# A two-layer hybrid trunk on one core: closing norm with its offsets laid into the result first and rows added by their stores, two row blocks' statistics on ScalarE, the last gating ahead of the last weight splits

## The chip, the cores and the metric

The kernel runs on one core of one Trainium2 chip. The metric is the device time of one execution in microseconds (us); the median of three runs before the change is 1376.93 us (1375.47 to 1379.27). Engines are named as in the profile: PE is TensorE, DVE is VectorE, ACT is ScalarE, POOL is GpSimd, SP is the queue that issues the plain transfers.

## What is computed

512 tokens of width 1024 pass through two layers. Each layer is a mixer (sparse attention beside a short convolution) and a feed-forward part, each closed by a layer norm of ALPHA times its input plus its output. The first layer's feed-forward is dense; the second one's is a mixture of 8 experts of which each token takes the best two. The end of the second layer is what the change touches:

```python
def layer_norm(x, g, b):
    mu = jnp.mean(xf, -1, keepdims=True)
    var = jnp.mean(jnp.square(xf - mu), -1, keepdims=True)
    return ((xf - mu) * lax.rsqrt(var + LN_EPS) * g + b)
...
def moe_swiglu(h, w_router, wg, wu, wd):
    out = jnp.zeros_like(h)
    for e in range(N_EXPERTS):
        out = out + gate[..., e:e + 1] * swiglu(h, wg[e], wu[e], wd[e])
    return out
...
        f = moe_swiglu(h, ...)
        h = layer_norm(ALPHA * h + f, ln2_g[l], ln2_b[l])
    return h
```

## The kernel before

All matrix work is done in a split form: a weight block is copied to a short format (`whi`, on ACT) and what the copy loses is kept as a second block (`wlo`, on DVE, which needs `whi`); three products, high by high, high by low and low by high, then stand for one. `split16` does this for the experts' weights, with `split16_ops` issuing the two instructions.

In the second layer the tokens are routed, experts are sorted by how many tokens they have, and each expert gathers its tokens (`x` from `hbuf`), multiplies by `moe_wg` and `moe_wu` (`expert_up`, two column groups of 6 and 5 blocks of 128), gates (`expert_gate`, `expert_hidden`: `eg` is the gated product on DVE, `ehh` its short copy on ACT, `ehl` the remainder on DVE) and multiplies by `moe_wd` (`expert_down`, or `expert_down_rows` for experts of exactly 128 slots). An expert's rows are then added to `abuf`, a buffer in device memory that starts as the layer's input, by indirect transfers that add at their target (`add_rows`, issued by POOL). Each such transfer waits for the one before. `expert_out` prepares these rows for the experts with two chunks of slots: PE transposes four blocks into a bank, ACT scales the bank into `yr`, twice per chunk; both chunks use the banks named `mm` and `po`.

The last expert works differently. When its turn begins (`if last:` in `moe`), the other seven experts' sums are read back from `abuf`: four blocks of 128 rows into `h`, and the last expert's own rows by a gather into `xl`. While its final matrix work runs, DVE takes the statistics of the four blocks (`row_stats`, `bn_aggr`), one root on ACT serves all (`roots`), and `finish(0)` norms each block by two DVE instructions (`rows_scaled`: subtract the mean and multiply by the gain; multiply by the root and add the offset) and stores it plainly from SP. `last_rows` adds the last expert's product to `xl` and takes its statistics; these rows are normed after that and written over the stored ones by an indirect scatter (`out_dram<-xl,dst`), which waits for the four stores.

The order on each engine's queue is set by the recording layer: instructions stand in the order of their data and priorities, and `issue_after` holds one back until another has been placed.

Of the kernel before, what the change touches and what calls it, by code (L numbers as in the profile page):

```python
# [54 lines left out]
class Trunk:  # L55
# [562 lines left out]
    def route(self, l, mp):  # L618
# [9 lines left out]
        self.dst = mp.tile([128, NE, 2], I32, name="dst")  # L628
        self.sgate = mp.tile([128, NE, 2], F32, name="sgate")

    def route_tile(self, tt):
        nc = self.nc
        if tt == 0:
            self.xt = self.state.tile([128, KD, S], F32, name="xh")
            room = self.state.tile([128, KD * S], F32, name="xl")
            n16, n32 = NE * NT * CAP // 2, NT * CAPS[0]
            self.oh16 = room[:, 0:n16].bitcast(F16).rearrange("p (e t j) -> p e t j", e=NE, t=NT)
            self.oh32 = room[:, n16:n16 + n32].rearrange("p (t j) -> p t j", t=NT)
        xt = self.xt
        q = slice(tt * 128, tt * 128 + 128)  # L640
        if tt == NT - 1:
            self.first = [self.psum(tag) for tag in ("mm", "mm", "s")]
            for u in range(NT - 1):
                self.first_rows(u)
        for half in range(2):
            p = self.psum("tr")
            for k in range(4):
                kk = half * 4 + k
                nc.tensor.transpose(p[:, k * 128:(k + 1) * 128], self.h[:, tt, kk * 128:(kk + 1) * 128], self.ident)
            v = p.rearrange("p (k q) -> p k q", k=4)  # L650
            self.routed = [nc.scalar.activation(xt[:, half * 4:half * 4 + 4, q], v, AF.Copy)]
        p = self.psum("po")
        for k in range(KD):
            nc.tensor.matmul(p[:, 0:NE], xt[:, k, q], self.wr[:, k], start=k == 0, stop=k == KD - 1)
        lg, sel = self.lg[:, tt], self.selb[:, tt]
        nc.vector.tensor_copy(lg, p[:, 0:NE])
        other = lg[:, None, :].to_broadcast([128, NE, NE])
        own = lg[:, :, None].to_broadcast([128, NE, NE])
        a = self.small.tile([128, NE, NE], F32, name="ra", bufs=1)
        b = self.small.tile([128, NE, NE], F32, name="rb", bufs=1)  # L660
        nc.vector.tensor_tensor(a, other, own, op=OP.is_equal)
        nc.vector.tensor_tensor(a, a, self.nkeep8, op=OP.mult)
        nc.vector.tensor_tensor(b, other, own, op=OP.is_gt)
        nc.vector.tensor_tensor(a, a, b, op=OP.add)
        rank = self.small.tile([128, NE], F32, name="rank")
        nc.vector.tensor_reduce(rank, a, axis=AX.X, op=OP.add)
        nc.vector.tensor_scalar(sel, rank, 1.5, None, op0=OP.is_lt)

        p = self.psum("po")
        for u in range(tt + 1):  # L670
            nc.tensor.matmul(p[:, 0:NE], self.before if u == tt else self.ones, self.selb[:, u], start=u == 0, stop=u == tt)
        nc.vector.scalar_tensor_tensor(self.mark[:, tt], p[:, 0:NE], 1.0, sel, op0=OP.add, op1=OP.mult)
        self.routed.append(nc.vector.tensor_scalar(self.oh32[:, tt], self.slots[:, 0:CAPS[0]], self.mark[:, tt, 0:1], None,
                                                   op0=OP.is_equal))
        if tt == NT - 1:
            self.first_rows(tt)
# [151 lines left out]
    def split16_ops(self, st, hi, lo, n):  # L828
        nc = self.nc

        for c in (slice(0, n // 2), slice(n // 2, n)) if n > 1 and self.nblock < 3 else (slice(0, n),):
            nc.scalar.activation(hi[:, c], st[:, c], AF.Copy, scale=WS)  # L832
            self.low = nc.vector.scalar_tensor_tensor(lo[:, c], st[:, c], WS, hi[:, c], op0=OP.mult, op1=OP.subtract)  # L833

    def weights(self, name, i0, e, rows, cols):

# [31 lines left out]
    def expert_hidden(self, parts, g):  # L868
        nc = self.nc
        hh, hl = (self.mp.tile([128, 6 * CAP], F16, name=x, bufs=2) for x in ("ehh", "ehl"))  # L870
        for x, c in parts:
            nc.vector.scalar_tensor_tensor(g[:, c], x, HS / (XS * WS), g[:, c], op0=OP.mult, op1=OP.mult)
            nc.scalar.activation(hh[:, c], g[:, c], AF.Copy)
            nc.vector.tensor_tensor(hl[:, c], g[:, c], hh[:, c], op=OP.subtract)
        return hh, hl

    def expert_down(self, i0, e, f0, n, hh, hl, ys):
# [10 lines left out]
                             lambda k: (hi[:, k - k0, c], lo[:, k - k0, c], hh[:, r(k)], hl[:, r(k)]), k0, k1,  # L888
                             first=f0 + k0 == 0 and m == 0, last=f0 + k1 == NFE and m == nm - 1, shared=True)

    def expert_down_rows(self, i0, e, f0, n, hh, hl, ys, finish=None):

        held = []
        for k0 in range(0, n, 2):
            k1 = min(n, k0 + 2)
            src = self.weights("moe_wd", i0, e, slice((f0 + k0) * 128, (f0 + k1) * 128), slice(0, D))
            hi, lo = self.split16(self.eblock([128, k1 - k0, D], src))
            held += [(k0 + k, hi[:, k], lo[:, k]) for k in range(k1 - k0)]
            if finish is not None and 0 < k0 and k1 < n:
                continue  # L900
            for half, y in enumerate(ys):
                c = slice(half * 512, half * 512 + 512)
                for k, h, l in held:
                    r = slice(k * 128, k * 128 + 128)
                    for a, b in ((hh, h), (hl, h), (hh, l)):
                        self.nc.tensor.matmul(y, a[:, r], b[:, c], start=f0 + k == 0 and a is hh and b is h,  # L906
                                              stop=f0 + k == NFE - 1 and b is l)
                if finish is not None and k1 == n:
                    finish(half)
            held = []  # L910
# [27 lines left out]
    def expert_out(self, e, yt):  # L938
        nc = self.nc
        for r, (s, n) in enumerate(chunks(e)):  # L940
            yr = self.mp.tile([128, D], F32, name="yr", bufs=2)[0:n]
            for half in range(2):
                p = self.psum("po" if half else "mm")
                for k in range(4):
                    nc.tensor.transpose(p[0:n, k * 128:(k + 1) * 128], yt[:, half * 4 + k, s:s + n], self.ident)
                nc.scalar.activation(yr[:, half * 512:half * 512 + 512], p[0:n], AF.Copy, scale=self.sgate[0:n, e, r:r + 1])
# [17 lines left out]
    def moe(self, l):  # L964
        nc = self.nc
        mp = self.mp = self.pool("moe%d" % l)
        i0 = l // 2
        self.nblock = 0
        groups = [(0, 6), (6, 5)]
        xs = self.gather_t(0, None)  # L970
        self.aux = mp.tile([128, NT, NE, 5], F16, name="aux")
# [40 lines left out]
        for turn, e in enumerate(TURN):  # L1012
# [23 lines left out]
            mid = None if last else (lambda: nxt.extend(self.gather_t(after, xg)))  # L1036
            hid = self.expert_hidden(up("moe_wu", 1, mid=mid), gate)
            before, xs = (e, hid, ys), nxt

        with self.tc.issue_after(self.low.ins):  # L1040
            for tt in range(NT):
                nc.vector.bn_aggr(mv[:, tt], self.row_stats(self.h[:, tt]))
            rs = self.small.tile([128, NT, 1], F32, name="rs4")
            roots(rs, mv)
            nc.vector.tensor_tensor(self.bad[:, 0:NT], mv[:, :, 1], mv[:, :, 1], op=OP.not_equal)

        def finish(half):
            if half == 0:
                with self.tc.issue_after(self.low.ins):
                    for tt in range(NT):  # L1050
                        self.rows_scaled(self.h[:, tt], mv[:, tt, 0:1], rs[:, tt], gb)
                        self.store(tt)
            last_rows(half, ys[half])
        self.expert_down_rows(i0, final, *groups[1], *hid, ys, finish)

        nl, nh, xl = 128, 1, end[:, 2:3]
        mv2 = mp.tile([nl, nh, 2], F32, name="mv2")
# [135 lines left out]
```

## Time and profile before

| | |
|---|---|
| median of three runs | 1376.93 us |
| the profiled execution, its own time | 1376.29 us |
| its span, first to last instruction | 1374.5 us |
| PE busy | 1331.4 us (97%) |
| DVE busy | 865.7 us (63%) |
| ACT busy | 668.4 us (49%) |
| POOL busy | 76.5 us (6%) |
| share of PE in the chain that ended last | 90% |
| last product of the last `moe_wu` block ends | 1344.7 us |
| last expert's final scatter is issued | 1367.6 us |

The profiled execution took 1.8 us more than its span, and 0.6 us less than the median of the runs. Times on the trace are counted from the start of the span. The busy shares are means over the whole kernel; the last 30 us have other limits than the rest, and are read by themselves.

### The profile page before, as it was taken

To read this page: it belongs to the slowest core of one execution; us is meant where nothing else is said; L and a number is where in the kernel's file an instruction comes from. 1 tells how busy PE (TensorE), PEld (TensorE's weight loads), DVE (VectorE), ACT (ScalarE), POOL (GpSimd) and SP (SyncE) were. 2 spreads that over 40 slices of the span, in tenths; PEclk is the share of its full clock that TensorE was granted. 3 is DMA by queue.
4 is the path that set the end of the run, shared out by engine and by line. 5 is a ranking of instruction groups with operands and counts; after the bars stand their busy time and mean duration, and the time that the engine had idled before them with its cause. 6 is when DMAs were issued, how large, how long until landed. Compare 5 with 4: busy or idle time off the path is not lost.

```text
span 1374.5 us, 26819 instructions
## 1 busy us (share of the span) xinstructions
PE 1331.4 (97%) x11476; PEld 1156.4 (84%) x11476; DVE 865.7 (63%) x1250; ACT 668.4 (49%) x948; POOL 76.5 (6%) x85
## 2 busy tenths in 40 slices
PE   5999999999999999999999999999999999999994
PEld 5888788898888888888887888889999999999872
DVE  7567665743333332228566665759787787788897
ACT  3575543323223222113565444326677677687881
POOL 3000000000000000000000000101011011010130
PEclk9999999999999999999999999999999999999997
DMA  8442021332323223222552020758999899999992
GB/s 253 128 123 62 32 62 35 119 105 79 123 74 110 92 100 112 95 92 70 159 152 62 31 62 1 245 228 300 313 358 354 275 339 371 315 354 375 378 377 98
DMA packets 135806, 241.09 MB, mean 175 GB/s; under 512 B 10810, under 2 KB 80538, under 8 KB 135684
## 3 DMA queue, kind: packets, MB, share of 16 engines
q1 hardware_dynamic: 130868, 223.19, 47.7%
q0 software_dynamic: 4816, 16.17, 4.2%
q8 instruction: 90, 1.47, 0.4%
q14 instruction: 32, 0.26, 0.1%
HBM read 227.74 MB, written 11.68 MB: 174 GB/s over the span
## 4 chain that ended last, share of the span: by engine, by line
PE 90%; DVE 4%; DMA 2%; ACT 2%; issue 1%; SPq 0%; POOL 0%; POOLq 0%; ACTq 0%; DVEq 0%
PE mm L203 46%; PE s L203 16%; PE tr L203 10%; PE po L486 3%; PE s L504 2%; PE s L470 2%; PE s L378 1%; PE po L203 1%; PE tr L470 1%; PE tr L504 1%; PE s L906 1%; DVE h L961 1%; DMA abuf<-yr,dst 1%; DVE h L962 1%; DMA h<-abuf 1%
## 5 line engine op out<-in xcount | busy, mean ns | idle before, releaser
L203 PEld LDWEIGHTS <-whi 128*128 128x128 f16 x3872 | 311.5, 98 | 1.2
L147 ACT ACTIVATE whi<-stage 128x1024 fp32r<-128x1024 f32 x122 | 127.9, 1058 | 302.9 <-PE mm L203 187.4
L148 DVE TENSOR_TENSOR wlo<-stage,whi 128x1024 fp32r<-128x1024 f32 x118 | 143.6, 1223 | 195.2 <-ACT whi L147 192.8
L203 PE MATMUL mm<-xh,whi 128*128 128x512 f32 (+1 forms) x672 | 257.2, 383 | 0.3 <-DVE e L309 0.3
L203 PE MATMUL mm<-xh,wlo 128*128 128x512 f32 (+1 forms) x672 | 252.8, 376 | 0.4 <-DVE wlo L148 0.4
L203 PE MATMUL mm<-xl,whi 128*128 128x512 f32 (+1 forms) x672 | 252.0, 375 | 0.0
L833 DVE SCALAR_TENSOR_TENSOR wlo<-estage,whi 128x1536 f16<-128x1536 f32 (+4 forms) x106 | 201.7, 1918 | 37.4 <-ACT whi L832 37.3
L832 ACT ACTIVATE whi<-estage 128x1536 f16<-128x1536 f32 (+4 forms) x106 | 170.5, 1613 | 65.8 <-PE s L203 26.0
L203 PEld LDWEIGHTS <-wlo 128*128 128x128 f16 x1936 | 189.1, 98 | 0.0
L203 PEld LDWEIGHTS mm<-xh,wlo 128*128 128x128 f32 x672 | 126.8, 189 | 23.9 <-DVE wlo L148 0.6
L203 PEld LDWEIGHTS mm<-xh,whi 128*128 128x128 f32 x672 | 127.4, 190 | 21.7 <-issue 1.3
L203 PEld LDWEIGHTS mm<-xl,whi 128*128 128x128 f32 x672 | 127.1, 189 | 21.0
L203 PE MATMUL tr<-eh,whi 128*128 128x128 f16 (+6 forms) x704 | 133.0, 226 | 0.0
L203 PE MATMUL tr<-eh,wlo 128*128 128x128 f16 (+6 forms) x704 | 133.0, 226 | 0.0
L203 PE MATMUL tr<-el,whi 128*128 128x128 f16 (+6 forms) x704 | 133.0, 226 | 0.0
L203 PE MATMUL mm<-eh,whi 128*128 128x128 f16 (+6 forms) x704 | 132.3, 226 | 0.0
L203 PE MATMUL mm<-eh,wlo 128*128 128x128 f16 (+6 forms) x704 | 132.3, 226 | 0.0
L203 PE MATMUL mm<-el,whi 128*128 128x128 f16 (+6 forms) x704 | 132.3, 225 | 0.0
L833 DVE SCALAR_TENSOR_TENSOR wlo<-stage,whi 128x1536 f16<-128x1536 f32 (+5 forms) x56 | 102.5, 1840 | 22.3 <-ACT whi L832 22.2
L832 ACT ACTIVATE whi<-stage 128x1536 f16<-128x1536 f32 (+5 forms) x56 | 86.8, 1551 | 40.2 <-PE tr L203 15.6
L203 PE MATMUL s<-ehl,whi 128*128 128x160 f16 (+5 forms) x528 | 102.6, 228 | 0.0
L203 PE MATMUL s<-ehh,whi 128*128 128x160 f16 (+5 forms) x528 | 102.6, 228 | 0.0
(310 smaller groups left out, 2297.2 us busy)
## 6 DMA issues: line engine op xcount, KB each, us to landing
estage<-in_moe_wd_dram SPq DMA_DIRECT2D x29, 1024.0 KB, 7.6
stage<-in_w_in_dram SPq DMA_DIRECT2D x32, 512.0 KB, 5.2
estage<-in_moe_wu_dram SPq DMA_DIRECT2D x21, 768.0 KB, 8.5
estage<-in_moe_wg_dram SPq DMA_DIRECT2D x18, 768.0 KB, 7.0
stage<-in_ffn_wg_dram SPq DMA_DIRECT2D x11, 1024.0 KB, 5.4
stage<-in_ffn_wu_dram SPq DMA_DIRECT2D x11, 1024.0 KB, 5.1
stage<-in_ffn_wd_dram SPq DMA_DIRECT2D x11, 1024.0 KB, 4.9
stage<-in_moe_wd_dram SPq DMA_DIRECT2D x11, 1024.0 KB, 7.4
```

The source lines that it names most:

```text
L147: nc.scalar.activation(h, st, AF.Copy)
L148: (eng or nc.vector).tensor_tensor(o, st, h.bitcast(F32), op=OP.subtract)
L203: self.nc.tensor.matmul(p, a, b, start=first and n == 0, stop=last and n == total - 1, skip_group_check=shared)
L378: nc.tensor.matmul(ph[r:r + 64, 0:256], e2[kv][:, c].rearrange("p g n -> p (g n)"), w1s[c // 8][:, c % 8], start=c < 2, stop=c > 13, skip_ ...
L470: nc.tensor.transpose(q[:, k * 128:k * 128 + 128], flat[:, c:c + 128], self.ident)
L486: nc.tensor.matmul(po[g * 64:g * 64 + 64, i * 128:i * 128 + 128], v[:, j, c:c + 64], flat[:, k:k + 128], start=False, stop=lbr == 1 and j ...
L504: nc.tensor.matmul(sp[:, wide[i]], qs[:, a, g, qi[i]], keys[:, br, g, 0:wide[i].stop - wide[i].start], start=keys is ks and i == blocks[0] ...
L832: nc.scalar.activation(hi[:, c], st[:, c], AF.Copy, scale=WS)
L833: self.low = nc.vector.scalar_tensor_tensor(lo[:, c], st[:, c], WS, hi[:, c], op0=OP.mult, op1=OP.subtract)
L906: self.nc.tensor.matmul(y, a[:, r], b[:, c], start=f0 + k == 0 and a is hh and b is h, stop=f0 + k == NFE - 1 and b is l)
L961: self.nc.vector.scalar_tensor_tensor(x, x, mean, gb[0:m, 0], op0=OP.subtract, op1=OP.mult)
L962: self.nc.vector.scalar_tensor_tensor(x, x, rs, gb[0:m, 1], op0=OP.mult, op1=OP.add)
```

## The change

The closing norm of the four row blocks is done in another order. The offsets (`ln2_b`) are written into all 512 rows of the result by one plain transfer early in the program. Each block then gets (x - mean) * gain on DVE and a multiplication by its root on ACT, and is added to the result by an indirect transfer from POOL's queue that adds at its target (row numbers in the new tile `token`), where a plain store from SP stood. The statistics of blocks 2 and 3 move from DVE to ACT: a copy that also sums, a scaled negative of the sum, and a square that also sums. The roots are taken for two blocks at a time. The gating of the last expert's last column group is placed ahead of the second and third of its last weight splits. Apart from that, `expert_out` puts its second chunk into the `s` banks.

```diff
@@ route
+        self.token = mp.tile([128, NT], I32, name="token")
+        nc.gpsimd.iota(self.token, pattern=[[128, NT]], base=0, channel_multiplier=1)
+        b = t["ln2_b"][l]
+        nc.sync.dma_start(self.out[0], bass.AP(tensor=b.tensor, offset=b.offset, ap=[[0, S], [1, D]]))
@@ split16_ops
-            nc.scalar.activation(hi[:, c], st[:, c], AF.Copy, scale=WS)
-            self.low = nc.vector.scalar_tensor_tensor(lo[:, c], st[:, c], WS, hi[:, c], op0=OP.mult, op1=OP.subtract)
+            self.high = nc.scalar.activation(hi[:, c], st[:, c], AF.Copy, scale=WS)
+            with ExitStack() as ctx:
+                for ins in self.held:
+                    ctx.enter_context(self.tc.issue_after(ins.ins))
+                self.low = nc.vector.scalar_tensor_tensor(lo[:, c], st[:, c], WS, hi[:, c], op0=OP.mult, op1=OP.subtract)
@@ expert_down_rows
+            if first is not None and k0 == 0:
+                first()
@@ expert_out
-                p = self.psum("po" if half else "mm")
+                p = self.psum("s" if r else ("mm", "po")[half])
@@ moe
-        with self.tc.issue_after(self.low.ins):
-            for tt in range(NT):
-                nc.vector.bn_aggr(mv[:, tt], self.row_stats(self.h[:, tt]))
-            rs = self.small.tile([128, NT, 1], F32, name="rs4")
-            roots(rs, mv)
-            nc.vector.tensor_tensor(self.bad[:, 0:NT], mv[:, :, 1], mv[:, :, 1], op=OP.not_equal)
+        rs, nm = (self.small.tile([128, NT, 1], F32, name=x) for x in ("rs4", "nm4"))
+        up_done, hidden, main = self.low, self.rest, self.main
+
+        def row_sums():
+            with self.tc.issue_after(up_done.ins):
+                for tt in range(2):
+                    nc.vector.bn_aggr(mv[:, tt], self.row_stats(self.h[:, tt]))
+            self.held = (hidden,)
 
         def finish(half):
             if half == 0:
+
+                with self.tc.issue_after(self.high.ins), self.tc.issue_after(main.ins):
+                    for tt in (2, 3):
+                        junk = mp.tile([128, D], F32, name="yr", bufs=2)
+                        nc.scalar.activation(junk, self.h[:, tt], AF.Copy, accum_out=mv[:, tt, 0:1])
+                        nc.scalar.activation(nm[:, tt], mv[:, tt, 0:1], AF.Copy, scale=-1.0 / D)
+                        nc.scalar.activation(junk, self.h[:, tt], AF.Square, bias=nm[:, tt], accum_out=mv[:, tt, 1:2])
+                    nc.vector.tensor_scalar(mv[:, 2:4], mv[:, 2:4], 1.0 / D, None, op0=OP.mult)
+                    for tts in (slice(0, 2), slice(2, 4)):
+                        roots(rs[:, tts], mv[:, tts])
+                nc.vector.tensor_tensor(self.bad[:, 0:NT], mv[:, :, 1], mv[:, :, 1], op=OP.not_equal)
                 with self.tc.issue_after(self.low.ins):
                     for tt in range(NT):
-                        self.rows_scaled(self.h[:, tt], mv[:, tt, 0:1], rs[:, tt], gb)
-                        self.store(tt)
+                        x = self.h[:, tt]
+                        nc.vector.scalar_tensor_tensor(x, x, mv[:, tt, 0:1], gb[:, 0], op0=OP.subtract, op1=OP.mult)
+                        nc.scalar.activation(x, x, AF.Copy, scale=rs[:, tt])
+                        nc.gpsimd.indirect_dma_start(
+                            out=self.out[0], in_=x, in_offset=None, compute_op=OP.add,
+                            out_offset=bass.IndirectOffsetOnAxis(ap=self.token[:, tt:tt + 1], axis=0))
             last_rows(half, ys[half])
-        self.expert_down_rows(i0, final, *groups[1], *hid, ys, finish)
+        self.expert_down_rows(i0, final, *groups[1], *hid, ys, finish, row_sums)
+        self.held = ()
```

How the instructions stand now is shown at three places. A row is a source line, an operation, the written and read tiles and a size. First VectorE in the last expert's final stretch: `wlo` is a weight split, `eg` and `ehl` are the gating, `rs` the roots, `mv` the means, `h` the four blocks. Before:

```order
L955 BN_STATS st<-h 128x6
L833 SCALAR_TENSOR_TENSOR wlo<-estage,whi 128x2048
L1042 BN_AGGR mv_7452<-st 128x2
L833 SCALAR_TENSOR_TENSOR wlo<-estage,whi 128x2048
L872 SCALAR_TENSOR_TENSOR eg<-tr,eg 128x512
L872 SCALAR_TENSOR_TENSOR eg<-tr,eg 128x128
L982 RECIPROCAL rs_15109<-rs_15109 128x4
L1045 TENSOR_TENSOR bad<-mv_7452 128x4
L833 SCALAR_TENSOR_TENSOR wlo<-estage,whi 128x1024
L874 TENSOR_TENSOR ehl<-eg,ehh 128x512
```

and now:

```order
L841 SCALAR_TENSOR_TENSOR wlo<-estage,whi 128x2048
L1055 BN_AGGR mv_7455<-st 128x2
L880 SCALAR_TENSOR_TENSOR eg<-tr,eg 128x512
L880 SCALAR_TENSOR_TENSOR eg<-tr,eg 128x128
L882 TENSOR_TENSOR ehl<-eg,ehh 128x512
L882 TENSOR_TENSOR ehl<-eg,ehh 128x128
L841 SCALAR_TENSOR_TENSOR wlo<-estage,whi 128x2048
L841 SCALAR_TENSOR_TENSOR wlo<-estage,whi 128x1024
L992 RECIPROCAL rs_15096<-rs_15096 128x2
L1074 SCALAR_TENSOR_TENSOR h<-h,mv_7455,xl 128x1024
```

Both gating steps now stand ahead of the two last splits, and two blocks' statistics are gone from the rows ahead of them.

Next ScalarE in the same stretch, from the last weight split on. Before:

```order
L832 ACTIVATE whi<-estage 128x1024
L981 ACT_TABLE_LOAD
L981 ACTIVATE rs_15109<-mv_7452,eps 128x4
L873 ACTIVATE ehh<-eg 128x512
L873 ACTIVATE ehh<-eg 128x128
L981 ACTIVATE rs_15181<-mv_15178,eps 128x1
```

and now (`yr` takes a result that nobody reads, the sums go to `mv`; `nm` is the negative mean):

```order
L837 ACTIVATE whi<-estage 128x1024
L881 ACTIVATE ehh<-eg 128x512
L881 ACTIVATE ehh<-eg 128x128
L1064 ACTIVATE yr,mv_7455<-h 128x1024 x2
L1065 ACTIVATE nm_15097<-mv_7455 128x1
L991 ACT_TABLE_LOAD
L991 ACTIVATE rs_15096<-mv_7455,eps 128x2
L1066 ACTIVATE yr,mv_7455<-h,nm_15097 128x1024
L1065 ACTIVATE nm_15097<-mv_7455 128x1
L1066 ACTIVATE yr,mv_7455<-h,nm_15097 128x1024
L1075 ACTIVATE h<-h,rs_15096 128x1024
```

The gating copy moved ahead of the root, and the sums of blocks 2 and 3 stand between it and the first block's scaling (L1075).

Last GpSimd's queue at the end, with the semaphores that each row waits for. `DMASW0` to `DMASW7` are given in turn to the transfers of this queue: the four reads of `h` have 3 to 6, `xl` has 7, and what follows begins again at 0. Before:

```order
L1023 DMA h<-abuf 128x1024 [waits DMASW2_49]
L1023 DMA h<-abuf 128x1024 x3
L1024 DMA xl<-abuf,idx 128x1024 [waits DMASW7_49]
L1073 DMA out_dram<-xl,dst 512x1024 [waits DMAHW5_49,DMAHW4_49,DMAHW6_49,DMAHW3_49,DVE_49]
L1075 TENSOR_LOAD flag [waits DVE_49]
```

and now:

```order
L1034 DMA xl<-abuf,idx 128x1024 [waits DMASW7_49]
L1076 DMA out_dram<-h,token 512x1024 [waits DMAHW0_49,Activation_49]
L1076 DMA out_dram<-h,token 512x1024 [waits DMASW0_49,Activation_49]
L1076 DMA out_dram<-h,token 512x1024 [waits DMASW1_49,Activation_49]
L1076 DMA out_dram<-h,token 512x1024 [waits DMASW3_49,DMASW2_49,Activation_49]
L1100 DMA out_dram<-xl,dst 512x1024 [waits DMASW4_49,DMASW3_49,DVE_49]
L1102 TENSOR_LOAD flag [waits DVE_49]
```

The first add has semaphore 0, the second 1, the third 2, the fourth 3. Each add stands behind a wait for the add before, and the final scatter behind a wait for the fourth.

## Rows read from the trace of the kernel before

**Rows 1.** The page: busy time by engine, share of the span, instructions.
```profile
PE 1331.4 (97%) x11476; PEld 1156.4 (84%) x11476; DVE 865.7 (63%) x1250; ACT 668.4 (49%) x948; POOL 76.5 (6%) x85
```

**Rows 2.** Windows: start and end, length, busy by engine, clock, DMA share, GB/s.
```profile
1331.00:1342.00 11.00, 11.00 (x109) 7.24 (x107) 10.58 (x11) 8.22 (x6) 8.71 (x4) 1.00 1.00 390
1342.00:1350.00 8.00, 2.66 (x48) 2.48 (x45) 8.00 (x14) 3.29 (x5) 0.00 (x0) 0.99 0.10 39
1350.00:1364.00 14.00, 9.62 (x30) 3.35 (x30) 14.00 (x17) 0.54 (x2) 0.00 (x0) 0.74 0.37 151
1364.00:1374.50 10.50, 0.16 (x1) 0.08 (x1) 3.30 (x10) 0.29 (x1) 1.02 (x1) 0.50 0.11 44
```

**Rows 3.** Timeline of DVE, last 36 us: start, length, line, tiles, idle before.
```profile
1339.04 1.87 DVE L955 BATCH_NORM_STATS2 st<-h 128x6 f32<-128x512 f32 x3
...
1344.53 2.27 DVE L833 SCALAR_TENSOR_TENSOR wlo<-estage,whi 128x2048 f16<-128x2048 f32 x1
...
1349.00 0.88 DVE L872 SCALAR_TENSOR_TENSOR eg<-tr,eg 128x512 f32<-128x512 f32 x2
...
1351.94 2.47 DVE L961 SCALAR_TENSOR_TENSOR h<-h,mv,xl 128x1024 f32<-128x1024 f32 x2
```

**Rows 4.** Timeline of PE: last up product, first product after the gating.
```profile
1344.44 0.22 PE L203 MATMUL tr<-eh,wlo 128*128 128x128 f16 x1
1350.40 0.61 PE L906 MATMUL s<-whi,ehh 128*128 128x512 f16 x1 [5.74 <-ACT ehh L873]
```

**Rows 5.** Timeline of POOL: indirect transfers and the read of h.
```profile
1222.28 2.10 POOL L923 DMA_INDIRECT abuf<-yr,dst  x1 [26.11 <-ACT yr L946]
1231.77 2.54 POOL L923 DMA_INDIRECT abuf<-yr,dst  x1 [7.39 <-DMA abuf<-yr,dst]
...
1330.38 2.25 POOL L1023 DMA_DIRECT2D h<-abuf  x4 [9.36 <-DMA abuf<-yr,dst]
...
1367.59 1.02 POOL L1073 DMA_INDIRECT out_dram<-xl,dst  x1 [27.58 <-DVE flag L1069]
```

**Rows 6.** The chain that ended last, around the last add of before.
```profile
1318.64 11.44 DMA abuf<-yr,dst
1330.08 0.30 issue
```

**Rows 7.** Timeline of ACT in the closing stretch.
```profile
1344.04 1.28 ACT L981 ACT_TABLE_LOAD   x1
...
1349.71 0.83 ACT L873 ACTIVATE ehh<-eg 128x512 f16<-128x512 f32 x2 [2.46 <-DVE eg L872]
...
1364.37 0.29 ACT L981 ACTIVATE rs<-mv,eps 128x1 f32<-128x1 f32 x1 [13.83 <-DVE mv L1058]
```

**Rows 8.** ACT by line and form: busy us, mean ns of one, idle before.
```profile
L147 ACT ACTIVATE whi<-stage 128x1024 fp32r<-128x1024 f32 x122 | 127.9, 1058 | 302.9 <-PE mm L203 187.4 <-PE po L203 79.7 <-issue 15.1
...
L511 ACT ACTIVATION_READ_ACCUMULATOR p<-s,m 128x1 f32 x96 | 19.1, 199 | 0.0
```

**Rows 9.** Transfers by POOL, us to landing: all adds; single ones at 1195, 1249, 1368, 901.
```profile
abuf<-yr,dst POOLq DMA_INDIRECT x13, 9.3
...
x<-hbuf,idx POOLq DMA_INDIRECT x1, 6.7
...
x<-hbuf,idx POOLq DMA_INDIRECT x1, 7.8
...
out_dram<-xl,dst POOLq DMA_INDIRECT x1, 4.0
...
hbuf<-h POOLq DMA_DIRECT2D x1, 512.0 KB, 3.2
```

**Rows 10.** Who PE waited for, 960 to 1300 us: total, times, longest.
```profile
PE po L945 <- ACT yr L946: 1.9, 6, 0.3
```

**Rows 11.** SP's queue from 33.4 us on, and that stretch's window (columns: Rows 2).
```profile
42.26 0.99 SPq L138 DMA_DIRECT2D stage<-in_w_in_dram  x2
...
33.40:42.30 8.90, 8.90 (x77) 8.90 (x76) 3.58 (x6) 4.17 (x9) 0.00 (x0) 1.00 0.24 54
```

More of the change, by code (lines that the diff above doesn't have):

```diff
@@ L872, in expert_hidden @@
             nc.vector.scalar_tensor_tensor(g[:, c], x, HS / (XS * WS), g[:, c], op0=OP.mult, op1=OP.mult)
-            nc.scalar.activation(hh[:, c], g[:, c], AF.Copy)
-            nc.vector.tensor_tensor(hl[:, c], g[:, c], hh[:, c], op=OP.subtract)
+            self.main = nc.scalar.activation(hh[:, c], g[:, c], AF.Copy)
+            self.rest = nc.vector.tensor_tensor(hl[:, c], g[:, c], hh[:, c], op=OP.subtract)
         return hh, hl
@@ L889, in expert_down, with expert_down_rows @@
                              first=f0 + k0 == 0 and m == 0, last=f0 + k1 == NFE and m == nm - 1, shared=True)
-    def expert_down_rows(self, i0, e, f0, n, hh, hl, ys, finish=None):
+    def expert_down_rows(self, i0, e, f0, n, hh, hl, ys, finish=None, first=None):
         held = []
@@ L967, in moe @@
         i0 = l // 2
-        self.nblock = 0
+        self.nblock, self.held = 0, ()
         groups = [(0, 6), (6, 5)]
```

## The prediction

> **What bounds the kernel now.** I read the page first. PE is busy 97% of the span [rows 1], so over most of the kernel only what PE does or waits for counts. The change lies almost wholly behind that: I therefore cut the last 43 us into windows [rows 2]. Until 1342 us PE is full; from 1342 to 1350 DVE is busy 8.00 of 8.00 us while PE works 2.66, and from 1350 to 1364 DVE is again full. After 1364 hardly anything is busy. So the end is set by DVE's queue, then by one transfer. DMA engines are at 1.00 of their time until 1342 and at 0.10 to 0.37 later, which matters below.
>
> DVE's own rows show why. The last up product is over at 1344.44 + 0.22 = 1344.66 us, but the next product starts at 1350.40, after 5.74 us that ended with the gating's short copy [rows 4]. The gating stood in DVE's queue behind statistics that begin at 1339.04 and behind two splits, and began at 1349.00 [rows 3]. Then come the eight norm instructions from 1351.94 on, the last expert's rows, and the scatter, which POOL issues at 1367.59 once DVE is done [rows 5]. From that issue to the end of the span it takes 1374.5 - 1367.6 = 6.9 us; I keep this for the changed kernel, which ends with the same scatter.
>
> **The change part by part.**
>
> *Offsets laid in.* One plain transfer of 512 x 4 KB = 2 MB goes on SP's queue early in the first layer, ahead of the weight load that SP issues at 42.26 us. In the stretch ahead of that load DMA is busy 0.24 of the time and moves 54 GB/s, and PE is full throughout [rows 11]. At the 390 GB/s that the engines reach when full [rows 2], 2 MB take 5.4 us, and 8.9 us are there. I cost it at nothing; if it is read at half that rate, it delays one load by about 2 us. The row numbers are one small POOL instruction in POOL's long idle time: nothing.
>
> *Second chunk in other banks.* PE waited six times, 1.9 us in all, for ACT to empty the `po` bank between an expert's two chunks [rows 10]. With banks of their own the eight transposes stand together and that wait goes: -1.9 us on the stretch where PE is the bound, so everything behind comes 1.9 us earlier. Bounds 0 (another wait takes its place) and 1.9.
>
> *Gating first.* Of the statistics four halves and their two closings stay ahead of the gating on DVE. Three halves take 1.87 us, so four and one closing take about 2.6 from 1339.04; with one split of 2.2 us [rows 3] DVE is free at about 1344.0, just before the product's first bank is complete at about 1344.4. The gating then starts 4.6 us earlier than at 1349.00. With the same steps after it, ACT's copy (0.83 us from 1349.71 in the trace [rows 7]) ends at 1350.5 - 4.6 = 1345.9. PE no longer stands 5.7 us. With the two splits that now follow, one of 2.2 us and one of half that size, DVE is done at about 1350.
>
> *Statistics on ACT.* Here ACT gets work that it must end before it can scale the first block. A pass over 128x1024 costs 1.06 us, and reading a sum out 0.20 [rows 8]; I take 1.3 for each such pass. From 1345.9: two sums (2.6) to 1348.5, a small instruction (0.3) to 1348.8, the table load (1.28) to 1350.1, the root (0.3) to 1350.4 [rows 7]. Before, that table load lay in an idle time at 1344.04; its cover is gone, but DVE's splits end at about the same time, so it costs 0.4 at most. DVE makes the first block ready (1.2 us, half of the pair in rows 3) by 1351.7. ACT meanwhile squares, negates, squares (1.3 + 0.3 + 1.3), to 1353.3, and scales the first block (1.06), to 1354.4. With -1.9 us from the banks, POOL can issue the first add at 1352.5.
>
> *The rest of DVE and ACT.* On DVE four of the eight norm instructions leave (-4.8 us). From 1351.7 I add: second block 1.2, then last rows' first half 0.7 behind ACT's second square, two blocks 2.4, two statistics 1.2 and the second half 0.7, closing and two passes 2.8: 1361.5, and 1359.6 with the banks' gain. That is some 8 us before the present scatter at 1367.6. If this path set the end, the span would be 1359.7 + 6.9 = 1366.6. PE's 30 products [rows 2] fit beside it.
>
> *Adds instead of stores.* Four stores by SP, beside DVE's work, become four adds on POOL's queue. By the order of the built program each waits until the one before has landed, and the final scatter, queued behind them on POOL, waits for the fourth. So the scatter's issue is not at DVE's end but at 1352.5 + 4P, with P the time from one add's issue to the next. The kernel before shows P when DMA is full: the 128-row add takes 11.44 us to land and 0.30 to the next issue [rows 6], and the thirteen have a median of 9.3 [rows 9]; from 1222.28 to 1231.77 two follow at 9.5 [rows 5]. In the closing stretch DMA is nearly idle, and no add was run there. Bounds: from above 11.7; from below the quiet scatter, 4.0 + 0.3 = 4.3, or even the quiet plain copy, 3.2 + 0.3 = 3.5 [rows 9]. What load costs I read from gathers, which don't add: 128 rows took 6.7 and 7.8 us in full traffic, the quiet scatter 4.0 [rows 9]. By ratio (4.0/7.25) the add falls from 11.4 to 6.3 us, by difference (3.25) to 8.2. An add reads and writes its target, and POOL spends 2.1 to 2.5 us on issuing one against 1.0 for the scatter [rows 5], so it can't be as fast as the scatter. I take 6.7, nearer to the ratio because waiting behind other traffic is the larger part, and P = 7.0.
>
> The Trainium skill ("DMA: Bandwidth & Descriptors", section "Anatomy of one DMA — SWDGE (gpsimd) path") gives a fit of about 2.0 us plus bytes over 436 GB/s for one such transfer, an estimate of 3.2 us for 512 KB. The quiet plain copy at 3.2 us agrees [rows 9], the adds do not; by the page the span would be about 1373.4, no change.
>
> *Sum.* Scatter issued at 1352.5 + 4 x 7.0 = 1380.5; end of span 1380.5 + 6.9 = 1387.4, which is 12.9 us more than 1374.5. The profiled execution's own time, 1376.29, becomes 1389.2; it lay 0.6 us under the median, so the forecast for the median is 1376.93 + 12.9 = **1389.8 us**, 0.9% slower.
>
> **The rivals.** About 0.3% (4.1 us) is what a measurement of this kernel can tell from no change.
>
> 1. *Adds in a quiet chip cost what a plain transfer costs.* P = 3.5 to 4.3: span 1352.5 + 14 + 6.9 = 1373.4 to 1376.6, -1.1 to +2.1 us, 1375.8 to 1379.0: the same. For it: the quiet copies in rows 9. Against it: POOL's time per add and the 4 us between loaded adds and loaded gathers. It decides below P = 4.8.
> 2. *The adds do not hold each other up* and follow at POOL's 2.1 us each. Then 1352.5 + 8.4 = 1360.9, just behind DVE's 1359.6, and the span is 1368: -6.5 us, 1370.4, faster. Against it stand the waits in the built order, and in the trace the second add of a pair and the read of `h` were released by a landing [rows 5, 6]. It needs P below 2.8.
> 3. *The adds stay as slow as under load.* P = 9.6 to 11.7: span 1397.8 to 1406.2, 23 to 32 us more, 1400 to 1409. For it: it is the only add that was measured. Against: DMA busy 1.00 then, 0.1 to 0.4 now [rows 2].
> 4. *Something between 1 and the forecast*, P = 4.8 to 5.6: 1381 to 1384.
>
> **How the numbers follow.** Forecast, P from 5.6 to 8.6 (1384.2 to 1396.2): 0.65. Rival 1: 0.10. Rival 2: 0.06. Rival 3 and what lies between it and the forecast: 0.14. Rival 4: 0.05. The range leaves out rival 2, half of rival 1 and the upper half of rival 3, 0.06 + 0.05 + 0.07 = 0.18: from 1379 to 1402. Faster 0.06, same 0.10, slower 0.65 + 0.14 + 0.05 = 0.84.
>
> **What would show it.** POOL's timeline should have four adds about 7 us apart, each released by the one before, the first near 1352.5, and the final scatter released by the fourth's landing, not by DVE. PE should start the last products near 1344 instead of 1350.4. DVE should be done near 1360 and then idle for some 20 us. PE's six waits for ACT at the transposes should be gone. I am wrong if the adds land in 4 us or less, if they overlap, or if the scatter is released by DVE; if the first add comes several us later than 1352.5, ACT's passes were costed too low.

## The result, and the profile after

The changed kernel takes 1392.25 us (median of six runs, 1390.15 to 1396.28) against 1378.7 us of the kernel before (six runs, 1375.47 to 1379.27): a ratio of 1.0108, with a 95% interval of 1.0093 to 1.0123. It is slower by about 13.5 us; 12.9 us were forecast. The profiled execution took 1393.74 us, with a span of 1391.8 us. Trace against trace the span grew by more, 17.3 us (1374.5 to 1391.8), since the profiled execution lay 2.4 us under its median before and 1.5 us above it after.

GpSimd's queue at the end, in the timeline of the changed kernel (start, length, line, tiles, idle time before and what ended it), shows the place:

```profile
1332.73 2.25 POOL L1033 DMA_DIRECT2D h<-abuf  x4 [9.32 <-DMA abuf<-yr,dst]
1335.29 7.10 POOL L1034 DMA_INDIRECT xl<-abuf,idx  x1 [0.30 <-issue]
1356.72 2.51 POOL L1076 DMA_INDIRECT out_dram<-h,token  x1 [14.33 <-ACT rs L991]
1364.59 1.55 POOL L1076 DMA_INDIRECT out_dram<-h,token  x1 [5.36 <-DMA out_dram<-h,token]
1371.45 1.55 POOL L1076 DMA_INDIRECT out_dram<-h,token  x1 [5.31 <-DMA out_dram<-h,token]
1378.25 1.55 POOL L1076 DMA_INDIRECT out_dram<-h,token  x1 [5.25 <-issue]
1385.06 1.01 POOL L1100 DMA_INDIRECT out_dram<-xl,dst  x1 [5.26 <-issue]
```

The first add is issued when ScalarE has scaled the first block. Then the steps are 7.87, 6.86, 6.80 and 6.81 us: issue to issue, with GpSimd idle for over 5 us in each until the add before has landed. The four adds' row of the transfers (count, median us from issue to landing) is

```profile
out_dram<-h,token POOLq DMA_INDIRECT x4, 6.1
```

and one by one they land 7.1, 6.1, 6.1 and 6.0 us after their issue; some 0.8 us pass from a landing to the next issue. The final scatter goes out at 1385.06 instead of the 1367.59 in [rows 5]. "issue" as the releaser of the last two means that the profile names no event; the built order has the same wait for each.

VectorE has long been done by then. Three of its rows in the changed kernel, the gating, the first block and the very last instruction:

```profile
1347.62 0.84 DVE L880 SCALAR_TENSOR_TENSOR eg<-tr,eg 128x512 f32<-128x512 f32 x2
...
1353.18 1.27 DVE L1074 SCALAR_TENSOR_TENSOR h<-h,mv,xl 128x1024 f32<-128x1024 f32 x1
...
1364.16 0.14 DVE L1096 CAST flag<-tr 1x1 int32<-1x1 f32 x1
```

From 1364.3 to 1385.06, 20.8 us, no engine but GpSimd has anything to do. The windows answer to [rows 2] (start and end, length, busy by engine PE, PEld, DVE, ACT, POOL, clock, DMA share, GB/s):

```profile
1342.00:1350.00 8.00, 5.95 (x94) 5.10 (x92) 6.18 (x12) 4.75 (x7) 0.40 (x1) 0.99 0.41 152
1350.00:1364.00 14.00, 7.77 (x29) 3.06 (x27) 13.90 (x24) 10.09 (x18) 2.51 (x1) 0.74 0.25 39
1364.00:1374.50 10.50, 0.00 (x0) 0.00 (x0) 0.30 (x2) 0.00 (x0) 3.10 (x2) 0.50 0.44 62
1374.50:1391.80 17.30, 0.00 (x0) 0.00 (x0) 0.00 (x0) 0.00 (x0) 2.56 (x2) 0.50 0.39 81
```

ScalarE went from 0.54 us of 14 to 10.09, VectorE stayed full to 1364, and behind it the adds stand alone. What PE waited for from 960 us on is now

```profile
PE tr L1094 <- DVE badb L1092: 5.4, 1, 5.4
PE s L916 <- ACT ehh L881: 1.9, 1, 1.9
```

so the six waits of [rows 10] are gone, and the wait for the gating fell from the 5.74 us of [rows 4] to 1.9.

### The profile page after: what moved, and what is told of

Read it like the earlier page. It is cut to its first block, busy times and chain, and to the rows that moved or that the text cites. A ratio compares the mean times of both kernels' runs of the same rounds, so it can differ in the third digit from the quotient of the medians.

```text
span 1391.8 us, 26828 instructions
## 1 busy us (share of the span) xinstructions
PE 1334.9 (96%) x11476; PEld 1160.0 (83%) x11476; DVE 859.0 (62%) x1243; ACT 676.6 (49%) x963; POOL 83.4 (6%) x90
## 5 line engine op out<-in xcount | busy, mean ns | idle before, releaser
L203 PE MATMUL s<-ehh,wlo 128*128 128x160 f16 (+5 forms) x528 | 102.6, 228 | 0.0
```

What stands on the lines that cost most here:

```text
L203: self.nc.tensor.matmul(p, a, b, start=first and n == 0, stop=last and n == total - 1, skip_group_check=shared)
```

## The experiments

All are the changed kernel with one edit, if not said otherwise; `...` marks what is left out of an edit. Ratios are to the kernel before, in runs on the same chip. A kernel without a ratio was run once. The experiments were run on several chips, so medians of different experiments compare less well than their ratios.

**Adds that do not wait for each other.**

```diff
...
-                        nc.gpsimd.indirect_dma_start(
-                            out=self.out[0], in_=x, in_offset=None, compute_op=OP.add,
-                            out_offset=bass.IndirectOffsetOnAxis(ap=self.token[:, tt:tt + 1], axis=0))
+                        nc.gpsimd.dma_start(self.out[0, tt * 128:(tt + 1) * 128], x, accum_op=OP.add)
```

> The four adds are made plain transfers that add at their target, each into its own 128 rows of the result, so that none waits for another; the last scatter still waits for all four. Theory (the chain of waits is the price): adds are issued as the blocks are scaled, at about 1356.4, 1357.7, 1360.2 and 1361.3 us of the changed kernel's trace, the fourth lands 7 to 8 us after its issue, the scatter goes out near 1369 instead of 1385.1, and the span falls by 12 to 16 us from 1391.8, to about 1376 to 1380. Rival (adding itself is the price, the engines do one add after the other in any case): issues come early but landings stay about 6.8 us apart, the scatter stays near 1385, the time within 3 us of the changed kernel's 1392. Second rival (GpSimd's issue is the price): issue spans grow beyond 5 us each.

Measured: 1379.22 us, ratio 1.0008 (0.9998 to 1.0017), span 1377.5. GpSimd's timeline:

```profile
1356.36 0.94 POOL L1074 DMA_DIRECT2D out_dram<-h  x1 [13.53 <-ACT rs L989]
1357.58 0.88 POOL L1074 DMA_DIRECT2D out_dram<-h  x1 [0.28 <-ACT h L1073]
1360.13 0.86 POOL L1074 DMA_DIRECT2D out_dram<-h  x1 [1.67 <-ACT h L1073]
1361.17 0.86 POOL L1074 DMA_DIRECT2D out_dram<-h  x1 [0.17 <-issue]
1370.80 1.04 POOL L1096 DMA_INDIRECT out_dram<-xl,dst  x1 [8.77 <-DMA out_dram<-h]
```

and the chain that ended last has the fourth add's landing:

```profile
1361.17 8.70 DMA out_dram<-h
```

Four adds took 1356.36 to 1369.87, 13.5 us, where the chain takes 28.3 (1356.72 to 1385.06). The chain of waits is the price of the change, as the theory said, and its numbers held within 2 us: the fourth add landed 8.7 us after its issue instead of 7 to 8, and the scatter went out at 1370.80 instead of near 1369. The edit also takes the row numbers away, and with them part of GpSimd's work (0.9 us of issue against 1.55 to 2.5). The rivals fall, though not wholly: the scatter still waits 7 us behind VectorE's end at 1363.9, so even free adds aren't hidden.

**Stores instead of adds.**

```diff
...
-        nc.sync.dma_start(self.out[0], bass.AP(tensor=b.tensor, offset=b.offset, ap=[[0, S], [1, D]]))
...
-                        x = self.h[:, tt]
-                        nc.vector.scalar_tensor_tensor(x, x, mv[:, tt, 0:1], gb[:, 0], op0=OP.subtract, op1=OP.mult)
-                        nc.scalar.activation(x, x, AF.Copy, scale=rs[:, tt])
-                        nc.gpsimd.indirect_dma_start(
...
+                        self.rows_scaled(self.h[:, tt], mv[:, tt, 0:1], rs[:, tt], gb)
+                        self.store(tt)
```

> The adds and the offsets' transfer are undone: each block is normed by two VectorE instructions and stored plainly, while the moved statistics, the early gating and the other banks stay. Theory: the adds are the whole loss, so the time falls from 1392 by about 16 us; VectorE has 4 x 1.2 = 4.8 us more than in the changed kernel, where it ended at 1364.2, so the scatter goes out near 1369 and the span is near 1376, about that of the kernel before (1374.5), within 0.3%. Rival (the moved statistics or the gating cost time by themselves): slower than the kernel before by over 4 us even without the adds.

Measured: 1377.96 us, ratio 1.0002 (0.9992 to 1.0012). The scatter is released by VectorE again:

```profile
1370.90 1.02 POOL L1092 DMA_INDIRECT out_dram<-xl,dst  x1 [25.94 <-DVE flag L1088]
```

Against the changed kernel that is -14.3 us, the 16 expected within 2: the adds and the offsets are more than the whole loss of 13.5 (by the ratios, which allow for the chip, 14.6 us). The rest of the change together comes out at nothing, which later runs take apart.

**The chain with plain writes.** The offsets are missing from its result.

```diff
-                            out=self.out[0], in_=x, in_offset=None, compute_op=OP.add,
+                            out=self.out[0], in_=x, in_offset=None,
```

> The four indirect transfers stay in their chain but write instead of adding, so the offsets are missing from the result (left out on purpose, as the timing of a plain indirect write is wanted). If adding makes each step slow, the step falls from 6.8 to the 4.0 to 4.5 us of the quiet scatter, the scatter goes out some 10 us earlier, near 1375, and the span is about 1382. If the step is a round trip that any indirect transfer from this queue pays, it stays at 6 to 7 us and the span within 3 us of 1392.

Measured: 1383.66 us. GpSimd:

```profile
1356.84 1.86 POOL L1076 DMA_INDIRECT out_dram<-h,token  x1 [13.50 <-ACT rs L991]
1361.86 1.77 POOL L1076 DMA_INDIRECT out_dram<-h,token  x1 [3.15 <-ACT rs L991]
1366.80 0.96 POOL L1076 DMA_INDIRECT out_dram<-h,token  x1 [3.18 <-DMA out_dram<-h,token]
1371.26 0.96 POOL L1076 DMA_INDIRECT out_dram<-h,token  x1 [3.50 <-issue]
1375.34 0.98 POOL L1100 DMA_INDIRECT out_dram<-xl,dst  x1 [3.12 <-issue]
```

The steps are 5.0, 4.9, 4.5 and 4.1 us, 18.5 in all. So of the 28.3 us of chain about 9.8 are for adding, and 18.5 are what a plain indirect write behind a wait costs on a quiet chip. Both matter. Without adding a step takes 4.6 us on average: a little over rival 1's 3.5 to 4.3, and still under the 4.8 below which the forecast let that rival decide. The Trainium skill ("DMA: Bandwidth & Descriptors", section "Anatomy of one DMA — SWDGE (gpsimd) path") fits a DMA by 2.0 us and its bytes over 436 GB/s, an estimate of 3.2 us for these 512 KB. The plain writes of this run landed 4.2, 4.2, 3.7 and 3.3 us after their issue, so the last of them agrees, and the adds of the changed kernel in 6.0 to 7.1, which do not; the measured times decide.

**Adds into four buffers of their own** (indirect, as in the changed kernel). The four blocks of the result are left unwritten.

```diff
...
-                            out=self.out[0], in_=x, in_offset=None, compute_op=OP.add,
+                            out=self.side[tt][:, :], in_=x, in_offset=None, compute_op=OP.add,
```

> The same indirect adds, but each into a buffer of its own in device memory, so that none waits for another and the last scatter for none of them; the result's four blocks are not written (left out). Theory (the chain is the price): the scatter goes out when VectorE is done, near 1364.5, and the span is about 1371 to 1373, or some us more if the end waits for the last add's landing. Rival (the engines do adds one after the other): the landings are 6 to 7 us apart and the program's end waits for the last one near 1385, so the span stays near 1390.

Measured: 1377.35 us, span 1375.5.

```profile
1354.63 2.50 POOL L1077 DMA_INDIRECT side<-h,token  x1 [13.51 <-ACT rs L992]
1357.43 1.56 POOL L1077 DMA_INDIRECT side<-h,token  x1 [0.30 <-issue]
1359.29 1.55 POOL L1077 DMA_INDIRECT side<-h,token  x1 [0.30 <-ACT h L1076]
1361.15 2.42 POOL L1077 DMA_INDIRECT side<-h,token  x1 [0.30 <-issue]
1363.87 1.01 POOL L1101 DMA_INDIRECT out_dram<-xl,dst  x1 [0.30 <-DVEq L1104]
```

With no wait between them the same indirect adds are issued 1.9 to 2.8 us apart, and the scatter at 1363.87. So the chain is the price for indirect adds as well as for plain ones. Yet the scatter hardly lands sooner, 18.1 us after the first add's issue against 18.3 in the first experiment: the transfers' row

```profile
out_dram<-xl,dst POOLq DMA_INDIRECT x1, 8.9
```

says 8.9 us to landing where [rows 9] has 4.0, behind the adds that the DMA engines still have to do. The windows of the first experiment while its four plain adds are under way, and of one plain write in the run without adding (columns as in [rows 2]):

```profile
1358.00:1369.80 11.80, 0.16 (x1) 0.08 (x1) 5.80 (x14) 2.48 (x3) 2.19 (x3) 0.50 0.91 174
```

```profile
1368.40:1369.50 1.10, 0.00 (x0) 0.00 (x0) 0.00 (x0) 0.00 (x0) 0.00 (x0) 0.50 1.00 402
```

The DMA engines are about full in both, but the adds move 174 GB/s and the write 402. That is the last part of the answer: the chain costs most, and adding itself fills the engines for some 3 us per block (11.8 us for four).

**Where the start came from.** The first add was issued at 1356.72, not at the forecast 1352.5, since GpSimd's read of `h` already stood at 1332.73 instead of the 1330.38 of [rows 5], not 1.9 us earlier than it. Set side by side, the two traces drift apart at two kinds of place: 2.4 us between 528 and 645 us, in the first layer's dense part, and 1.5 to 1.6 us each near 1087 and 1197 us, where the granted clock fell. The kernel before was therefore run and profiled once more, and the banks were tried by themselves:

> The kernel before, unchanged, profiled once more on the chip of this call. In the changed kernel and in the first four experiments the first layer's dense part, which the change does not touch, took some 2.4 us longer between 528 and 645 us than in the profile before, and TensorE's granted clock stood at its lower level for 3.4 us near 1087 and mostly near 1197 us, at unchanged work. If these are the chip's and the day's, this trace shows them too; if they come from the changed code, it shows neither.

```diff
-                p = self.psum("po" if half else "mm")
+                p = self.psum("s" if r else ("mm", "po")[half])
```

> Of the change only the second chunk's banks, in the kernel before. Forecast: PE's six waits for ScalarE at the transposes, 1.9 us, are gone and the last expert's read of its blocks starts 1.9 to 3.0 us earlier: 1374 to 1375.5 against 1377.4 to 1378. Rival: with the waits gone the stretches at the lower clock near 1087 and 1197 us appear, each worth about 1.6 us, and the time stays within 1 us of the kernel before.

The second profiled execution of the kernel before took 1380.34 us; its dense part was as in the first. The banks alone: 1376.01 us, ratio 0.9991 (0.9982 to 0.9999). The windows from 1080 to 1092 us of that execution and of the banks alone:

```profile
1080.00:1092.00 12.00, 12.00 (x118) 10.81 (x116) 4.85 (x5) 4.84 (x6) 1.92 (x2) 0.86 0.83 265
```

```profile
1080.00:1092.00 12.00, 12.00 (x120) 10.85 (x118) 5.41 (x6) 5.00 (x6) 1.92 (x2) 0.86 0.70 216
```

A mean of 0.86 is a part of the stretch at 1.2 GHz and the rest at 2.4: in the changed kernel the granted clock is 0.51 from 1086.9 to 1090.4 us, 1.00 before and behind it, and PE is busy throughout. One of the two traces of the kernel before has it too, so the change is not needed for it. Whether it favours it is not settled: all nine traces with the new banks show a lower clock near 1087 us, of the four with the old banks one. PE's gain from the banks adds up to some 3.0 us in the trace and 1.4 in the median; the forecast for them, 1.9 to 3.0 less, was too high, and the rival's "within 1 us" too low.

**Two adds and two stores**, with the new and with the old banks. The two adds are plain transfers into their own rows, as in the first experiment.

```diff
...
+                        if tt >= 2:
+                            self.rows_scaled(x, mv[:, tt, 0:1], rs[:, tt], gb)
+                            self.store(tt)
+                            continue
...
```

> Blocks 0 and 1 are added by plain transfers that don't wait for each other, blocks 2 and 3 normed on VectorE and stored plainly; the rest as in the changed kernel. If the adds' transfer time (four unchained adds landed over 11.6 us in the plain-add experiment) was what held the scatter there, two adds land by about 1364 and VectorE sets the end, some 2.4 us shorter than with stores alone: scatter near 1368 less the drift, 1374 to 1376.5 against 1377.4 for before. If the shared cost lies in VectorE's order and not in the adds, it stays at 1378, as with stores.

> As the run with two adds and two stores, but with the second chunk's banks of the kernel before. If the new banks bring 1.9 to 3.0 us, this is slower than that run by as much; if lower clock near 1087 and 1197 us takes it back, the two are alike and the lower clock is absent here.

Measured: 1376.04 us, ratio 0.9986 (0.9977 to 0.9995), and with the old banks 1377.42 us, ratio 1.0002 (0.9991 to 1.0013). The banks are worth 1.4 us here too. With the new banks VectorE and the scatter:

```profile
1365.05 0.14 DVE L1096 CAST flag<-tr 1x1 int32<-1x1 f32 x1
```

```profile
1368.21 1.04 POOL L1100 DMA_INDIRECT out_dram<-xl,dst  x1 [10.86 <-DMA out_dram<-h]
```

The time came out as expected, but not for the reason given: VectorE did not set the end. In the chain that ended last stands the landing of the second plain store:

```profile
1360.55 6.82 DMA out_dram<-h
```

It took 6.8 us, where the result's transfers took 2.7 to 4.0 in the run with stores alone, and the scatter went out 3.0 us behind VectorE's end. The second add landed 9.7 us after its issue, at 1366.2, so the stores stood beside the adds in DMA engines that were full (a share of 1.03 from 1358 to 1363 us). Two adds are still too many.

**The addresses.** The kernels with the longer dense part all hold the new small tile `nm4` in the pool `small`, which stands ahead of the first layer's tiles. It makes that pool 128 bytes larger, and what lies behind it, `hh` and `hl` among it, moves by 128 bytes. Three runs test that; the first two move `nm4` to another pool (the second of them also adds block 0 alone, by a plain transfer, and stores the other three), the third puts such a tile, unused, into the kernel before:

```diff
-        rs, nm = (self.small.tile([128, NT, 1], F32, name=x) for x in ("rs4", "nm4"))
+        rs, nm = (p.tile([128, NT, 1], F32, name=x) for p, x in ((self.small, "rs4"), (mp, "nm4")))
```

> The changed kernel, with the small tile nm4 (the negative means) taken from another pool, so that the first layer's dense part has its tiles (hh, hl) at the addresses of the kernel before again, 128 bytes lower. All seven traces of kernels that hold the tile in the first pool show that part some 2.4 us longer, the three without it do not. If the addresses do that, the stretch from 528 to 645 us is as in the kernel before and the time falls from 1392 by about 2.4 us to 1389.5 to 1390; the chain of adds stays. Rival (some other part of the change does it, as the order on an engine): the stretch stays 2.4 us longer.

> Block 0 alone is added (a plain transfer), blocks 1 to 3 are normed on VectorE and stored, and the small tile is moved. With two adds the stores waited behind them in the DMA engines and the scatter for a landing, 3.2 us after VectorE's end. With one add VectorE should set the end again: 1.2 us more of it than with two adds, the scatter some 2 us earlier, and 2.4 us less in the first layer if the addresses do that: 1371.5 to 1373.5 against 1377.4 for the kernel before. If the stores still land late behind the add, or the addresses do nothing, 1374 to 1376.

```diff
             rs = self.small.tile([128, NT, 1], F32, name="rs4")
+            nc.gpsimd.memset(self.small.tile([128, NT, 1], F32, name="nm4"), 0.0)
```

> The kernel before with one unused 16-byte tile of four buffers (128 bytes) added to the first pool, set to zero once by GpSimd, so that hh and hl move by 128 bytes and nothing else changes. If the addresses make the first layer's dense part longer, the stretch from 528 to 645 us takes 2.4 us more and the time is 1379.5 to 1380 against 1377.4. If not, the time is that of the kernel before.

Measured: the changed kernel with the tile moved 1389.22 us, ratio 1.0077 (1.0063 to 1.0091); the kernel before with the tile 1380.2 us, ratio 1.0020 (1.0010 to 1.0029). PE in the window from 560 to 620 us, in the kernel before, in the changed kernel, in that with the tile moved, and in the kernel before with the tile (the first number in brackets counts PE's products):

```profile
560.00:620.00 60.00, 60.00 (x267) 49.67 (x266) 13.48 (x11) 11.83 (x12) 0.00 (x0) 1.00 0.27 95
```

```profile
560.00:620.00 60.00, 60.00 (x260) 48.66 (x259) 13.48 (x11) 11.67 (x11) 0.00 (x0) 1.00 0.30 101
```

```profile
560.00:620.00 60.00, 60.00 (x267) 49.68 (x266) 13.49 (x11) 11.83 (x12) 0.00 (x0) 1.00 0.28 92
```

```profile
560.00:620.00 60.00, 60.00 (x260) 48.67 (x259) 13.48 (x11) 11.67 (x11) 0.00 (x0) 1.00 0.30 100
```

In the same 60 us, at a full clock in all four, PE does 267 products or 260. By line and form one product's mean goes from 389 to 395 ns:

```profile
L203 PE MATMUL s<-whi,hh 128*128 128x512 f32 x33 | 12.8, 389 | 0.0
```

```profile
L203 PE MATMUL s<-whi,hh 128*128 128x512 f32 x32 | 12.6, 395 | 0.0
```

The tile's place does it, in both directions: in the built programs of the two kernels with the longer part `hh` lies 128 bytes further on than in the other two. Which of the moved tiles it is, and why, was not tried.

With the tile moved, the changed kernel's GpSimd rows answer the forecast's sum more closely than those of the changed kernel itself:

```profile
1353.07 2.50 POOL L1076 DMA_INDIRECT out_dram<-h,token  x1 [13.51 <-ACT rs L991]
1360.78 1.55 POOL L1076 DMA_INDIRECT out_dram<-h,token  x1 [5.20 <-DMA out_dram<-h,token]
...
1380.96 1.01 POOL L1100 DMA_INDIRECT out_dram<-xl,dst  x1 [5.24 <-issue]
```

The kernel with one add and the tile moved has the lowest ratio found, though not clear of the 0.9986 with two adds: 1374.86 us, ratio 0.9976 (0.9965 to 0.9987), faster than both the kernel before and the changed one. It is some 2 us short of what I had expected from it, in the range given for the case that the stores land late or the addresses do nothing. Neither holds: PE does 266 products in the 60 us, and in its trace VectorE sets the end, as it should:

```profile
1366.47 1.03 POOL L1100 DMA_INDIRECT out_dram<-xl,dst  x1 [10.42 <-DVE flag L1096]
```

but the window from 1080 to 1092 us has a clock of 0.72, the lowest of these traces there.

## Why the prediction was right, point by point

- **The chain of adds (the deciding step): right, in kind and size.** P was forecast at 7.0 us and is 7.1 on average (28.34 over four). The two bounds were 3.5 and 11.7; reading the load's share from gathers by ratio, and staying a little above, hit it, with some luck: a landing takes 6.3 us on average, the ratio's own figure and not the 6.7 taken, and from a landing to the next issue it takes 0.8 us and not 0.3, so two errors cancel. With the waits gone the time falls by 13.0 us in the first experiment, with the adds gone by 14.3 in the second (by the ratios 13.8 and 14.6).
- **What the adds cost beside the wait: left out.** Rival 2 took adds without waits to cost GpSimd's issue alone, 2.1 us each. Without waits four of them need 13.5 us to land, so that rival's 1370.4 us was out of reach even had its condition held: the runs without waits gave 1379.2 with plain adds and 1377.4 with indirect ones.
- **ScalarE's new work: right, the exact sum by luck.** From the read of `h` to the first add 24.0 us were forecast (1330.4 to 1354.4), and 23.99 measured (1332.73 to 1356.72). In the seven other traces with this work it is 22.9 to 23.4. The gating's copy ended 16.4 us behind the read instead of 15.5, and shorter passes behind it made that up. The first add came 4.2 us later than 1352.5, which the prediction named as a sign of passes costed too low; they were not, the whole delay stands already in the read of `h`. A pass over 128x1024 with its sum is 1.04 + 0.19 us, forecast 1.3:

```profile
1349.03 1.04 ACT L1064 ACTIVATE yr<-h 128x1024 f32<-128x1024 f32 x1
1349.97 0.19 ACT L1064 ACTIVATION_READ_ACCUMULATOR yr<-h 128x1 f32 x1
...
1351.31 1.28 ACT L991 ACT_TABLE_LOAD   x1
...
1355.31 1.13 ACT L1075 ACTIVATE h<-h,rs 128x1024 f32<-128x1024 f32 x1
```

- **Gating first: right, and worth little while something else ends last.** PE's wait for it fell from 5.74 to 1.9 us (1.1 in the run with the tile moved). With stores in the adds' place the scatter hangs on VectorE, which is rid of two blocks' statistics but keeps all eight norm instructions: from the read of `h` to the scatter that run takes 35.4 us, the four traces with the old order 36.8 to 39.2.
- **The banks: a term mis-sized, with bounds that did not hold all of it.** I took -1.9 us from PE's waits, with bounds of 0 and 1.9. By the starts of GpSimd's transfers the gap to the kernel before closes by about 0.5 us at each of six experts, some 3.0 in all, and the median falls by 1.4 (two pairs of runs). The lower clock near 1087 and 1197 us, which the sum has no term for, takes some 3.1 us in the changed kernel's trace, and so undoes the gain there.
- **The offsets' transfer: right.** It cost nothing, though it came at about the rate that the prediction had doubts of (212 GB/s, and 15.4 us to landing): near 188 us the same GpSimd instruction starts at 188.69 before and at 188.70 after. In the changed kernel the stretch of [rows 11] has a DMA share of 0.99 instead of 0.24 and PE is still full:

```profile
33.40:42.30 8.90, 8.90 (x76) 8.90 (x76) 3.44 (x5) 4.00 (x9) 0.00 (x0) 1.00 0.99 212
```

- **The step that was missing: the addresses.** The sum has no term for a new tile moving others; it is +2.4 us between the two traces. With this term taken away the scatter was issued at 1380.96 against a forecast of 1380.5, and the span was 1387.3 against 1387.4. Part of that is luck too, as the banks' gain and the lower clock cancel in this trace as well; by the medians on one chip this kernel is 11.5 us slower than the kernel before, where 12.9 were forecast.
- **The end after the scatter: right**, 6.9 forecast, 1391.8 - 1385.06 = 6.7 measured.

So the size of the sum rests on the chain, and its closeness to the measured 13.5 us in part on terms that cancel. Set together, by medians but for the addresses: the adds +14.3 us (against stores), the addresses +2.4, the banks -1.4, and a remainder of -1.8 for gating and statistics give the measured 13.5. That last number is only the difference of the others. No run has gating and statistics alone; the 35.4 us above, against 36.8 and more, show a gain of 1.4 us or more in the last stretch.

## What to carry to other kernels

Transfers that are taken to overlap in their target wait for each other, and then the number of them times issue-to-landing is a chain of its own: read it from the waits in the built order and price it with the landing of the same kind of transfer, not with a store's. Moving work off a full engine pays only until the new path is as long as the old one; here one block by a plain add was hidden, two were not, and four in a chain cost 13 us. A new small tile can move large ones, so compare traces far from the edit too.

## What the runs showed of the hardware that was not expected

- An indirect transfer of 128 rows that adds at its target has a step of 6.8 to 7.9 us behind a wait where hardly any other transfer is under way, one that writes 4.1 to 5.0. Four plain adds without waits land within 13.5 us, with the DMA engines at 0.91 of their time and 174 GB/s (a plain write: 402), and other transfers queue behind them: behind four indirect adds the scatter's landing went from 4.0 to 8.9 us.
- 128 bytes of shift in the place of all tiles behind the small pool, `hh` and `hl` among them, made the products of the first layer's second dense part 1.5% longer by their mean (389 to 395 ns) and 2.6% fewer per time (267 to 260 in 60 us); 2.4 us, or 0.2% of the kernel. Which tile it is stays open.
- TensorE's granted clock fell for short stretches in the middle of full work, near 1087 us in ten of thirteen traces, one of the two of the kernel before among them.
